# Gate product of the small experts in two weight streams, gathers for two experts at once, and a router in a written order, in a two-layer decoder trunk with a top-2-of-8 expert layer

## Chip, core and metric

The kernel runs on one core of a Trainium2 chip. The metric is the device time of one execution in microseconds (us); the kernel before stands at 1468.9 us, the median of three runs (1468.63 to 1469.94). A change under about 0.2% (2.9 us) can't be told from none.

## The reference, cut to what matters

Two layers over 256 tokens of width 1024 in float32. Each has attention (two head groups) with an output projection `w_out` and a residual, then a feed-forward part: dense SwiGLU in layer 0, top-2-of-8 SwiGLU experts of inner width 3584 in layer 1. The change touches the expert layer and the end of the attention before it:

```python
v = rmsnorm(h, ffn_norm[layer])
h = h + moe_swiglu(v, router_w, exp_w_gate, exp_w_up, exp_w_down)

def moe_swiglu(h, router_w, w_gate, w_up, w_down):
    logits = (hf @ router_w).astype(jnp.float32)
    top_logit, top_e = lax.top_k(logits, TOP_K)
    gate = jax.nn.softmax(top_logit, axis=-1)
    ...
    # each token: the sum over its two experts e of
    #   gate_e * ((silu(x @ w_gate[e]) * (x @ w_up[e])) @ w_down[e])
```

All 8 experts' weights, 336 MiB, are read whatever the routing is. With these inputs four experts (0, 1, 2 and 4) have at most 64 tokens and four (3, 5, 6 and 7) have 65 to 128.

## The kernel before, in words

**Precision.** A float32 operand is split into a rounded part `hi` (type F32R, which TensorE streams in one pass) and a remainder `lo`. A product is then three F32R products: `xh*wh`, `xl*wh`, `xh*wl` (`product3`, lines 406 to 410). The splitting is done on the chip: ScalarE (ACT) writes `whi`, VectorE (DVE) writes `wlo = raw - whi`.

**The weights' stream.** `Flow` (lines 110 to 138) hands the expert layer its weights in 336 pieces of 1 MiB, each 128 x 2048. SyncE's queue (SP) loads them into a ring of `DEEP` = 9 raw buffers (four of tag `raw`, and `x6`, `x5`, `x3`, `x7`, `x4`, which the attention before uses for other things). `flow.hi()` issues the next piece's ACT instruction (line 125), `flow.lo()` the DVE instruction (line 132) and then the load of the piece that takes over the raw buffer. There are 4 `hi` and 3 `lo` buffers.

**Steps.** The expert layer walks through 56 steps, 8 experts by 7 chunks of 512 inner columns, in an order written by hand (`tc.manual_schedule`, from line 1037): each engine executes its instructions in this order. A step (e, c) has six pieces of weights: two halves of the gate, two of the up matrix, and two of the down matrix of the step before. TensorE (PE) computes `eg` (gate) and `eu` (up), ACT takes Silu of `eg`, DVE multiplies (`esg`), PE does the two `down` halves of the step before into `ey`, then turns `esg` (`turn`, tile `eT`), and ACT and DVE split the result into `eth`.

**Few tokens.** A tile has 128 rows. An expert with at most 64 tokens has each token in two slots, s and s + 64. A matmul whose 128 stationary columns are `MIX` = 64:192 of [hi | lo] then has `lo` in the one half and `hi` in the other, so that two matmuls a weight tile (`x_mix*wh`, `x_mix*wl`) take the place of three; the two halves of the result still have to be added. `by_number` (lines 960 to 965) puts both versions into PE's program with a branch on the expert's count. `eu` and `ey` have the two-stream form (lines 979 to 982; `turn` adds the halves with the 0/1 matrix `both`). `eg` always has the three-stream one, because Silu needs the whole sum.

**Gather.** An expert's tokens are gathered by a float32 matmul of a part of `hg` (h times the norm's gain) with the 0/1 matrix `so` (`gather`, lines 894 to 902; 8 column blocks by 2 token tiles, 128 columns each), at chunks 3 and 4 of the expert before; ACT and DVE then split the result into `xe`. `slots`, `rstd_of` and `place` make `so`, the rows' norm factors and the matrix that scatters the results back; finished experts are scattered in pairs (`scatter`, `gain_of`) during the next expert.

**Router.** `to_moe` and its `after` (lines 1211 to 1224) run at the end of the attention, after each column group of the last projection: they turn h (`turn_h`) and write `hg`. `moe` then computes the logits `lg` (lines 833 to 836), the top two (`max`, `max_index`), places by 0/1 matmuls (`rk`, `count`), the norm factors (`row_rstd`), and gathers expert 0. This part's order was found by the scheduler of the framework, and the loads and splits of the first weights run beside it.

Of the kernel before, what the change touches and what calls it, by code (L numbers as in the profile page):

```python
# [21 lines left out]
S = 256  # L22
NT = 2
# [27 lines left out]
DEEP = N_RAW + 5  # L51
# [90 lines left out]
def trunk_kernel(ctx: ExitStack, tc: tile.TileContext, T: dict, out: bass.AP):  # L142
# [81 lines left out]
    later = ("x6", "x5", "x3", "x7", "x4")  # L224
# [604 lines left out]
    def moe(l, mpool, ht, hg):  # L829

        wg = mpool.tile([128, KD, NE], F32, name="wg")
        dve.tensor_tensor(out=wg, in0=wr, in1=column(R_FN + l * KD, KD).unsqueeze(2).to_broadcast([128, KD, NE]), op=ALU.mult)
        lb = [mm_bank("lg")[:, 0:NE] for _ in range(NT)]
        for k in range(KD):
            for t in range(NT):
                pe.matmul(lb[t], ht[:, k, t * 128:(t + 1) * 128], wg[:, k, :], start=(k == 0), stop=(k == KD - 1))

# [3 lines left out]
        for t in range(NT):  # L841
            dve.max(out=mx[:, t, :], in_=lb[t])
            dve.max_index(out=ix[:, t, :], in_max=mx[:, t, :], in_values=lb[t])
        fx = mpool.tile([128, NT, 8], F32, name="fx")
        dve.tensor_copy(fx, ix)
# [5 lines left out]
        one = [mpool.tile([128, NT, NE], F32, name=f"one{i}") for i in range(2)]  # L851
        sel = mpool.tile([128, NT, NE], BF16, name="sel")
        for i in range(2):
            dve.tensor_tensor(out=one[i], in0=ie, in1=per_expert(fx[:, :, i]), op=ALU.is_equal)
        dve.tensor_tensor(out=sel, in0=one[0], in1=one[1], op=ALU.add)

        rb = tr_bank("rk")
        pe.matmul(rb[:, 0:NE], before, sel[:, 0, :], start=True, stop=True)
        pe.matmul(rb[:, NE:2 * NE], ones, sel[:, 0, :], start=True, stop=False)
        pe.matmul(rb[:, NE:2 * NE], before, sel[:, 1, :], start=False, stop=True)  # L860
        pos = mpool.tile([128, NT, NE], F32, name="pos")
        dve.scalar_tensor_tensor(out=pos, in0=rb[:, 0:2 * NE].rearrange("p (t e) -> p t e", t=NT), scalar=1.0, in1=sel,
                                 op0=ALU.add, op1=ALU.mult)


        cb = tr_bank("count")
        for t in range(NT):
            pe.matmul(cb[:, 0:NE], ones, sel[:, t, :], start=(t == 0), stop=(t == NT - 1))
        few = mpool.tile([128, NE], F32, name="few")
        dve.tensor_scalar(out=few, in0=cb[:, 0:NE], scalar1=64.0, scalar2=None, op0=ALU.is_le)  # L870
        number = mpool.tile([128, NE], I32, name="number")
        dve.tensor_copy(number, cb[:, 0:NE])
        most = mpool.tile([128, 1], F32, name="most")
        dve.tensor_reduce(out=most, in_=cb[:, 0:NE], axis=AX.X, op=ALU.max)
        again = tri
        dve.memset(again[:, 0:64], 0.0)
        dve.memset(again[:, 64:128], -64.0)
        both = mpool.tile([128, 128], F32, name="both")
        for i in range(2):
            dve.tensor_tensor(out=both[:, i * 64:(i + 1) * 64], in0=ident[:, 0:64], in1=ident[:, 64:128], op=ALU.add)  # L880
        rs = row_rstd(h, D, "h")

        def slots(e):

            so = mpool.tile([128, NT, 128], F32, name="so", tag="so", bufs=2)
            own = so[:, 0, :]
            dve.scalar_tensor_tensor(out=own, in0=again, scalar=few[:, e:e + 1], in1=slot, op0=ALU.mult, op1=ALU.add)
            for t in reversed(range(NT)):
                dve.tensor_scalar(out=so[:, t, :], in0=own, scalar1=pos[:, t, e:e + 1], scalar2=None,
                                  op0=ALU.is_equal)  # L890
            x = main.tile([128, KD, 2, 128], F32R, name="xe", tag=("ulo", "uhi")[e % 2])
            held[e] = [so, x]

        def gather(e, k):

            so, x = held[e][:2]
            b = tr_bank("ga")
            for j in range(4):
                f = slice((k + j) * 128, (k + j + 1) * 128)
# [11 lines left out]
        def rstd_of(e):  # L911

            so = held[e][0]
            b = tr_bank("rl")
            for t in range(NT):
                pe.matmul(b[:, 0:1], so[:, t, :], rs[:, t:t + 1], start=(t == 0), stop=(t == NT - 1))
            rl = mpool.tile([128, 1], F32, name="rl", tag="rl", bufs=2)
            dve.tensor_copy(rl, b[:, 0:1])
            held[e] += rl, pe.value_load(number[0:1, e:e + 1], min_val=0, max_val=S)
# [3 lines left out]
        slots(0)  # L923
        for k in (0, 4):
            x = gather(0, k)
            upper(*x)
            lower(*x)
        rstd_of(0)
        gt = mpool.tile([128, 2, NT], F32, name="gt")
        dve.tensor_tensor(out=gt[:, 1, :], in0=mx[:, :, 1], in1=mx[:, :, 0], op=ALU.subtract)  # L930
        dve.tensor_tensor(out=gt[:, 1, :], in0=gt[:, 1, :], in1=rs, op=ALU.mult)
        act.activation(gt[:, 1, :], gt[:, 1, :], AF.Exp)
        dve.tensor_scalar(out=gt[:, 0, :], in0=gt[:, 1, :], scalar1=1.0, scalar2=None, op0=ALU.add)
        dve.reciprocal(out=gt[:, 0, :], in_=gt[:, 0, :])
        dve.tensor_tensor(out=gt[:, 1, :], in0=gt[:, 1, :], in1=gt[:, 0, :], op=ALU.mult)
        gte = mpool.tile([128, NT, NE], F32, name="gte")
        for i in range(2):
            dve.tensor_tensor(out=one[i], in0=one[i], in1=per_expert(gt[:, i, :]), op=ALU.mult)
        dve.tensor_tensor(out=gte, in0=one[0], in1=one[1], op=ALU.add)
# [14 lines left out]
        flag = mpool.tile([128, 1], I32, name="flag")  # L954
        dve.tensor_scalar(out=flag, in0=most, scalar1=-128.0, scalar2=0.0, op0=ALU.add, op1=ALU.max)
        over = nc.values_load(flag[0:1, 0:1], min_val=0, max_val=128)

        acc = [mpool.tile([128, D], F32, name=f"acc{t}") for t in range(NT)]

        def by_number(e, many, few):  # L960

            with tc.If(held[e][3] > 64) as cond:
                many()
            with cond.Else():
                few()
# [5 lines left out]
        def terms(e, x, mix, steps):  # L971
# [7 lines left out]
            def few():  # L979
# [9 lines left out]
        def up(e, x, b, half, mix):  # L989
            terms(e, x, mix, [(b, k, wh, wl, k == 0, k == KD - 1) for k, (wh, wl) in enumerate(flow.take(), half * 4)])  # L990

        def down(e, c, ht, y, half):
            terms(e, ht, True, [(y[n], half * 2 + i, wh[:, n * 512:(n + 1) * 512], wl[:, n * 512:(n + 1) * 512],
# [3 lines left out]
        def turn(e, hc):  # L997
# [6 lines left out]
            def few():  # L1004
# [3 lines left out]
            by_number(e, many, few)  # L1008
# [12 lines left out]
        def scatter(c, t, first, pair):  # L1021
            f = slice(c * 512, (c + 1) * 512)
            b = tr_bank("scat")
            for i, (st, yhl) in enumerate(pair):
                for j in range(2):
                    pe.matmul(b, st[:, t * 128:(t + 1) * 128], yhl[:, j, f], start=(i + j == 0), stop=(i + j == 2))
# [9 lines left out]

        with tc.manual_schedule():
            prev = None
            for _ in range(N_HI):
                flow.hi()  # L1040
            for _ in range(N_LO):
                flow.lo()
            for step in seq + [None]:
                e, c = step or (NE, 0)
                if step:
                    _, x, rl, _ = held[e]
                    b = mm_bank("eg")
# [12 lines left out]
                    up(e, x, b, 0, True)  # L1060
                    flow.hi()
                    flow.lo()
                    up(e, x, b, 1, True)
# [3 lines left out]
                if prev:  # L1067
# [6 lines left out]
                    g = None  # L1074
# [3 lines left out]
                    if step:  # L1078
# [4 lines left out]
                    if step:  # L1083
                        lower(ht, b)
                    if g:
                        upper(*g)
                        lower(*g)
                    if pc == last:
                        st, gs = pair[-1]
                        yhl = main.tile([128, 2, D], F32R, name="yhl", tag=f"x{1 + pe_ % 2}")  # L1090
# [200 lines left out]
```

## Time and profile before

| what | before |
|---|---|
| median of 3 runs | 1468.9 us (1468.63 to 1469.94) |
| the profiled execution: its own time / its span | 1466.53 us / 1464.7 us |
| busy PE / DVE / ACT | 97% / 81% / 67% of the span |
| HBM read | 434.45 MB, 297 GB/s over the span |
| chain that ended last | PE 85%, DMA 9%, DVE 3%, ACT 2%, issue 1% |
| granted TensorE clock, mean | 0.993 |

The span runs from the first to the last instruction of the profiled execution. A busy PE is one with matmuls in flight, which is not the same as one at its peak. The expert layer covers the span from about 500 us on. The profile has two records for one float32 matmul, and one for an F32R matmul.

### The profile page before, as it was taken

The page shows a single profiled execution, that of the slowest core. Times are in us where ns is not written, and L with a number is a line of the kernel's source. Part 1 is how long each engine was busy: PE and PEld are TensorE (multiplying, and loading weights), DVE is VectorE, ACT ScalarE, POOL GpSimd, SP SyncE. Part 2 cuts the span into 40 slices and gives each one's busy share as a digit, 9 for nine tenths or more (in the row PEclk, how much of TensorE's full clock was granted, in tenths as well). Part 3 has the DMA queues.
Part 4 walks back from the last instruction along what each step waited for, and adds up shares of the span by engine and source line. Part 5 has one row for each costly group of instructions (what it writes and reads, how often), then busy time and mean ns, then how long its engine had stood idle before and what let it go on. Part 6 is the DMA issues. An engine that isn't in the chain of part 4 may idle for free.

```text
span 1464.7 us, 19495 instructions
## 1 busy us (share of the span) xinstructions
PE 1422.1 (97%) x7166; PEld 1165.2 (80%) x7166; DVE 1190.8 (81%) x1395; ACT 986.8 (67%) x1013; POOL 15.2 (1%) x21
## 2 busy tenths in 40 slices
PE   7999999999999889999999999999999999999997
PEld 6787888888887768877868778888888888888885
DVE  5776755555777679999999998889999888889885
ACT  5556644444665458888788787778787677677773
POOL 2000000000000000000000000000000000000000
PEclk9999999999999889999999999999999999999999
DMA  8922455657725469999999999999999999999990
GB/s 274 315 87 87 144 188 172 218 166 235 251 91 179 150 242 384 395 393 391 394 395 393 393 394 394 393 384 391 393 393 394 384 367 366 326 339 357 365 348 31
DMA packets 201063, 437.72 MB, mean 299 GB/s; under 512 B 9464, under 2 KB 26096, under 8 KB 200944
## 3 DMA queue, kind: packets, MB, share of 16 engines
q1 hardware_dynamic: 198304, 435.16, 81.8%
q8 instruction: 81, 1.33, 0.4%
q10 hardware_dynamic: 2176, 0.52, 0.2%
q0 software_dynamic: 464, 0.40, 0.1%
q14 instruction: 38, 0.31, 0.1%
HBM read 434.45 MB, written 1.08 MB: 297 GB/s over the span
## 4 chain that ended last, share of the span: by engine, by line
PE 85%; DMA 9%; DVE 3%; ACT 2%; issue 1%; SPq 0%; DVEq 0%; ACTq 0%
DMA raw<-in_exp_w_up_dram 7%; PE eg L408 6%; PE eg L410 6%; PE eg L409 6%; PE ey L409 3%; PE ey L410 3%; PE ey L408 3%; PE eu L410 3%; PE eu L409 3%; PE eu L408 3%; PE pj L410 3%; PE pj L408 3%; PE pj L409 3%; PE y L408 2%; PE ey L982 2%; PE eu L981 2%
## 5 line engine op out<-in xcount | busy, mean ns | idle before, releaser
L132 DVE TENSOR_TENSOR wlo<-raw,whi 128x2048 fp32r<-128x2048 f32 x336 | 758.4, 2287 | 56.1 <-PE ey L410 19.4
L125 ACT ACTIVATE whi<-raw 128x2048 fp32r<-128x2048 f32 x336 | 639.1, 1915 | 102.3 <-PE eu L409 26.6
L93 DVE TENSOR_TENSOR wlo<-raw,whi 128x1024 fp32r<-128x1024 f32 (+1 forms) x130 | 154.7, 1193 | 107.2 <-ACT whi L92 102.1
L92 ACT ACTIVATE whi<-raw 128x1024 fp32r<-128x1024 f32 (+1 forms) x130 | 133.5, 1032 | 116.9 <-PE y L409 41.8
L408 PE MATMUL eg<-whi,xe 128*128 128x512 f32 x448 | 181.8, 406 | 0.0
L410 PE MATMUL eg<-wlo,xe 128*128 128x512 f32 x448 | 177.2, 396 | 0.1
L409 PE MATMUL eg<-whi,xe 128*128 128x512 f32 x448 | 177.1, 395 | 0.0
L410 PEld LDWEIGHTS eg<-wlo,xe 128*128 128x128 f32 x448 | 84.2, 188 | 20.7 <-DVE wlo L132 0.5
L409 PEld LDWEIGHTS eg<-whi,xe 128*128 128x128 f32 x448 | 84.4, 188 | 17.8
L408 PEld LDWEIGHTS eg<-whi,xe 128*128 128x128 f32 x448 | 84.4, 188 | 17.6
L982 PE MATMUL ey<-wlo,eth 128*128 128x512 f32 x224 | 89.3, 398 | 2.7 <-DVE wlo L132 2.1
L982 PE MATMUL eu<-wlo,xe 128*128 128x512 f32 x224 | 89.1, 398 | 2.3 <-DVE wlo L132 2.1
L410 PE MATMUL eu<-wlo,xe 128*128 128x512 f32 x224 | 88.7, 396 | 1.2 <-DVE wlo L132 1.2
L981 PE MATMUL eu<-whi,xe 128*128 128x512 f32 x224 | 88.8, 396 | 0.0
L409 PE MATMUL eu<-whi,xe 128*128 128x512 f32 x224 | 88.6, 395 | 0.0
L408 PE MATMUL eu<-whi,xe 128*128 128x512 f32 x224 | 88.6, 395 | 0.0
L408 PE MATMUL ey<-whi,eth 128*128 128x512 f32 x224 | 87.9, 392 | 0.7 <-ACT eth L905 0.7
L981 PE MATMUL ey<-whi,eth 128*128 128x512 f32 x224 | 88.5, 395 | 0.0
L409 PE MATMUL ey<-whi,eth 128*128 128x512 f32 x224 | 87.5, 390 | 0.2 <-DVE eth L908 0.2
L410 PE MATMUL ey<-wlo,eth 128*128 128x512 f32 x224 | 87.5, 391 | 0.0
L905 ACT ACTIVATE eth<-eT 128x512 fp32r<-128x512 f32 x56 | 33.3, 595 | 71.9 <-PE eT L1002 50.2
L408 PE MATMUL pj<-whi,uhi 128*128 128x512 f32 (+1 forms) x192 | 74.7, 391 | 1.6 <-ACT qv L453 1.6
(318 smaller groups left out, 2386.1 us busy)
## 6 DMA issues: line engine op xcount, KB each, us to landing
raw<-in_exp_w_gate_dram SPq DMA_DIRECT2D x112, 1024.0 KB, 11.1
raw<-in_exp_w_up_dram SPq DMA_DIRECT2D x112, 1024.0 KB, 11.3
raw<-in_exp_w_down_dram SPq DMA_DIRECT2D x112, 1024.0 KB, 11.8
raw<-in_w_in_dram SPq DMA_DIRECT2D x20, 1024.0 KB, 6.0
raw<-in_ffn_w_gate_dram SPq DMA_DIRECT2D x10, 1024.0 KB, 5.1
raw<-in_ffn_w_up_dram SPq DMA_DIRECT2D x10, 1024.0 KB, 5.1
raw<-in_ffn_w_down_dram SPq DMA_DIRECT2D x10, 1024.0 KB, 5.0
raw<-in_cmp_w_dram SPq DMA_DIRECT2D x8, 1024.0 KB, 6.0
```

What stands on the lines that cost most here:

```text
L92: self.nc.scalar.activation(hi, src, AF.Copy)
L93: self.nc.vector.tensor_tensor(out=lo, in0=src, in1=hi.bitcast(F32), op=ALU.subtract)
L125: ws.nc.scalar.activation(hi, src, AF.Copy)
L132: self.ws.nc.vector.tensor_tensor(out=lo, in0=src, in1=hi.bitcast(F32), op=ALU.subtract)
L408: pe.matmul(dst, xh, wh, start=first, stop=False)
L409: pe.matmul(dst, xl, wh, start=False, stop=False)
L410: pe.matmul(dst, xh, wl, start=False, stop=last)
L905: act.activation(x[:, :, 0, :], b.rearrange("p (k t) -> p k t", k=4), AF.Copy)
L981: pe.matmul(b, x[:, k, MIX], wh, start=first, stop=False)
L982: pe.matmul(b, x[:, k, MIX], wl, start=False, stop=last)
```

## The change

- The gate has the two-stream form for small experts too. Its two matmuls a weight tile write into one fixed PSUM bank `gp`, cleared once; ACT copies it to `sg`; `whole`, a branch of its own after the first half of `eu`, multiplies `sg` by the 0/1 matrix `both` (float32, 512 columns), which adds the halves; Silu then reads that bank. The copy is issued for every expert, `whole` only runs for small ones.
- The gathers use h times gain split into two F32R parts, `hgh` and `hgl`, instead of a float32 `hg`: 4 matmuls a column block, whose results stand side by side as [hi | lo], so that one ACT copy an expert and block takes the place of the split by ACT and DVE. Experts are gathered in twos (0; 1 and 2; 3 and 4; 5 and 6; 7), 256 columns a matmul, two blocks a step at chunks 3 to 6 of the even experts. A third `xe` buffer takes the tag `x4`, and `DEEP` falls from 9 to 8.
- The router's order is written by hand; the logits' matmuls move to `after`, behind each column group of the last projection; the arithmetic of the experts' weights (`gates`) moves behind the first step; `acc` is `h` itself.
- Expert 6 is scattered by itself during expert 7, and expert 7 alone at the end. In the last step `turn` and its splits stand between the two `down` halves of the step before instead of behind them.

```diff
-DEEP = N_RAW + 5
+DEEP = N_RAW + 4
...
-    later = ("x6", "x5", "x3", "x7", "x4")
+    later = ("x6", "x5", "x3", "x7")
...
+        def slots(es):
+            n = len(es)
+            so = mpool.tile([128, NT, 2, 128], F32R, name="so", tag="so")
...
+                x = main.tile([128, KD, 2, 128], F32R, name="xe", tag=("ulo", "uhi", "x4")[e % 3])
...
+        def gather(pair_, k):
...
+            b = tr_bank("ga").rearrange("p (i e t) -> p i e t", i=2, e=2)
+            f = slice(k * 128, (k + 1) * 128)
+            for i in range(2):
                 for t in range(NT):
-                    pe.matmul(b[:, j * 128:(j + 1) * 128], hg[:, t, f], so[:, t, :], start=(t == 0), stop=(t == NT - 1))
-            return x[:, k:k + 4], b
+                    pe.matmul(b[:, i, 0:n, :], hg[i][:, t, f], so[:, t], start=(t == 0), stop=(t == NT - 1))
+            for i, x in enumerate(xs):
+                act.activation(x[:, k], b[:, :, i, :], AF.Copy)
...
-        def terms(e, x, mix, steps):
+        def terms(e, x, steps, part=None):
...
+            def fewer():
                 for b, k, wh, wl, first, last in steps:
+                    b = b if part is None else part
                     pe.matmul(b, x[:, k, MIX], wh, start=first, stop=False)
                     pe.matmul(b, x[:, k, MIX], wl, start=False, stop=last)
-            if mix:
-                by_number(e, many, few)
-            else:
-                many()
...
+            by_number(e, many, fewer)
...
+        def whole(e, b, part):
+            with tc.If(held[e][4] > 0):
+                pe.matmul(b, both, part, start=True, stop=True)
...
+        def router():
+            rstd = rstd_steps()
+            squares()
...
+            flow.hi()
+            flow.hi()
...
+            first_ = slots([0])
+            for k in range(4):
+                gather(first_, k)
+            next(rest)
+            flow.hi()
+            flow.lo()
+            next(rest)
+            for k in range(4, KD):
+                gather(first_, k)
+            for _ in rstd:
+                pass
+            flow.lo()
...
+            rstd_of(0)
...
+            flow.lo()
+            act.activation(gt[:, 1, :], gt[:, 1, :], AF.Exp)
+            flow.hi()
...
+            router()
+            gp = cmp_bank("gp")
+            dve.memset(gp, 0.0)
...
-                    up(e, x, b, 0, False)
+                    up(e, x, g, 0, gp)
                     flow.hi()
                     flow.lo()
-                    up(e, x, b, 1, False)
+                    up(e, x, g, 1, gp)
                     sg = mpool.tile([128, 512], F32, name="esg", tag="esg")
-                    act.activation(sg, b, AF.Silu, scale=rl)
+                    act.activation(sg, gp, AF.Copy)
...
-                    up(e, x, b, 0, True)
+                    up(e, x, b, 0)
+                    whole(e, g, sg)
+                    act.activation(sg, g, AF.Silu, scale=rl)
...
-                    if step and e + 1 < NE and c in (3, 4):
-                        g = gather(e + 1, (c - 3) * 4)
+                    final = step == seq[-1]
+                    if final:
+                        nxt, b = turn(e, sg)
+                        upper(nxt, b)
+                        lower(nxt, b)
+                    if step and e % 2 == 0 and c >= 3:
+                        for k in range((c - 3) * 2, (c - 2) * 2):
+                            gather(coming, k)
                     down(pe_, pc, ht, y, 1)
...
-                        if pe_ % 2:
+                        if pe_ % 2 or pe_ == NE - 2:
                             left.extend((n, t, pe_ == 1, pair) for n in range(2) for t in range(NT))
...
+                    if (e, c) == (0, 0):
+                        gates()
...
+                    if c == 2 and e % 2 == 0:
+                        coming = slots([i for i in (e + 1, e + 2) if i < NE])
...
             def after(c0, cw):
                 turn_h(c0, cw, ht)
-                f = slice(c0, c0 + cw)
-                for t in range(NT):
-                    dve.tensor_tensor(out=hg[:, t, f], in0=h[t][:, f], in1=row[:, f], op=ALU.mult)
+                for k in range(c0 // 128, (c0 + cw) // 128):
+                    for t in range(NT):
+                        pe.matmul(lb[t], ht[:, k, t * 128:(t + 1) * 128], wg[:, k, :], start=(k == 0), stop=(k == KD - 1))
+                if c0 + cw <= 512:
+                    list(scaled(slice(c0, c0 + cw)))
```

`scaled` is the split of h times gain: two DVE products and two ACT copies, then two DVE subtractions; for the second half of the columns `router` issues them (`next(rest)`).

## Rows read from the trace of the kernel before

**Rows 1.** Stretches: busy us (PE, PEld, DVE, ACT, POOL), PE clock, DMA share, GB/s

```profile
510.00:520.00 10.00, 2.82 (x18) 2.73 (x17) 8.76 (x39) 0.45 (x2) 0.00 (x0) 0.50 0.60 211
...
530.00:540.00 10.00, 7.96 (x38) 6.29 (x38) 8.37 (x6) 7.39 (x5) 0.00 (x0) 1.00 1.02 376
540.00:550.00 10.00, 10.00 (x52) 8.36 (x50) 9.26 (x6) 8.51 (x7) 0.00 (x0) 1.00 0.90 323
...
720.00:850.00 130.00, 126.33 (x583) 100.21 (x583) 124.58 (x79) 103.33 (x70) 0.00 (x0) 1.00 1.04 393
...
960.00:1080.00 120.00, 120.00 (x573) 99.45 (x572) 117.43 (x76) 97.48 (x67) 0.00 (x0) 1.00 1.04 389
...
1250.00:1300.00 50.00, 50.00 (x240) 41.28 (x239) 41.36 (x29) 33.35 (x25) 0.00 (x0) 1.00 0.93 326
```

**Rows 2.** Tile eu by line: L981 is the two-stream form, L408 the other

```profile
L981 PE MATMUL eu<-whi,xe x224: 390/398/496, 528.7 to 1069.8; 128*128 128x512 f32 x112
...
L408 PE MATMUL eu<-whi,xe x224: 392/394/398, 848.4 to 1439.4; 128*128 128x512 f32 x112
```

**Rows 3.** The chain that ended last, 740 to 1100 us: start, us, what

```profile
848.70 13.94 DMA raw<-in_exp_w_up_dram
...
967.21 0.44 PE eT L1002 x4
...
988.92 0.93 PE scat L1026 x4
...
1074.10 0.89 PE eT L1006 x8
```

**Rows 4.** The same chain, 1100 to 1436 us

```profile
1158.00 1.78 PE ga L901 x16
...
1411.54 0.44 PE eT L1002 x4
1428.63 0.44 PE eT L1002 x4
```

**Rows 5.** Groups of ACT, 540 to 1440 us: count, busy us, mean ns, idle before

```profile
L905 ACT ACTIVATE eth<-eT 128x512 fp32r<-128x512 f32 x54 | 32.1, 595 | 67.1 <-PE eT L1002 46.0 <-PE eT L1006 21.1
...
L949 ACT ACTIVATE st<-pl 128x256 fp32r<-128x256 f32 x8 | 3.0, 372 | 0.0
```

**Rows 6.** Timeline of SP's queue around the router

```profile
528.44 3.18 SPq L74 DMA_DIRECT2D raw<-in_exp_w_up_dram  x2
```

**Rows 7.** Timeline around the router and the first step: start, us, instructions

```profile
497.76 0.28 PE L410 MATMUL y<-wlo,pob 128*128 128x256 f32 x1
497.88 0.28 PE L408 MATMUL y<-whi,pob 128*128 128x256 f32 x1
...
503.29 6.74 PE L836 MATMUL lg<-wg,ht 128*128 128x8 f32 x32 [1.01 <-DVE wg L832]
...
515.34 0.17 DVE L855 TENSOR_TENSOR sel<-one,one 128x16 bf16<-128x16 f32 x1
...
517.49 5.30 PE L901 MATMUL ga<-so,hg_rows 128*128 128x128 f32 x32 [1.64 <-DVE y_h L324]
...
522.99 0.48 PE L408 MATMUL eg<-whi,xe 128*128 128x512 f32 x1
...
528.44 0.40 PE L410 MATMUL eg<-wlo,xe 128*128 128x512 f32 x1
528.67 0.39 PE L981 MATMUL eu<-whi,xe 128*128 128x512 f32 x1
```

**Rows 8.** Timeline of DVE, early in expert 0

```profile
546.80 6.68 DVE L132 TENSOR_TENSOR wlo<-raw,whi 128x2048 fp32r<-128x2048 f32 x3
```

**Rows 9.** The chain that ended last, its end: start, us, what

```profile
1446.83 0.70 DVE eth L908
...
1454.20 3.43 PE scat L1026 x13
...
1457.66 0.69 DVE acc L1030
```

More of the change, by code (lines that the diff above doesn't have):

```diff
@@ L826, in ffn, with moe @@
         return hi, lo
[L829 to L834, printed above, removed]
-            for t in range(NT):
-                pe.matmul(lb[t], ht[:, k, t * 128:(t + 1) * 128], wg[:, k, :], start=(k == 0), stop=(k == KD - 1))
+    def moe(l, mpool, lb, hg, rest):
         mx = mpool.tile([128, NT, 8], F32, name="mx")
         ix = mpool.tile([128, NT, 8], U32, name="ix")
-        for t in range(NT):
-            dve.max(out=mx[:, t, :], in_=lb[t])
-            dve.max_index(out=ix[:, t, :], in_max=mx[:, t, :], in_values=lb[t])
         fx = mpool.tile([128, NT, 8], F32, name="fx")
-        dve.tensor_copy(fx, ix)
+        one = [mpool.tile([128, NT, NE], F32, name=f"one{i}") for i in range(2)]
+        sel = mpool.tile([128, NT, NE], BF16, name="sel")
+        pos = mpool.tile([128, NT, NE], F32, name="pos")
+        few = mpool.tile([128, NE], F32, name="few")
+        number = mpool.tile([128, NE], I32, name="number")
+        small = mpool.tile([128, NE], I32, name="small")
+        most = mpool.tile([128, 1], F32, name="most")
+        flag = mpool.tile([128, 1], I32, name="flag")
+        both = mpool.tile([128, 128], F32, name="both")
+        gt = mpool.tile([128, 2, NT], F32, name="gt")
+        gte = mpool.tile([128, NT, NE], F32, name="gte")
+        acc = h
+        again = tri
         ie = iota.unsqueeze(1).to_broadcast([128, NT, NE])
@@ L849, in per_expert @@
             return v.unsqueeze(2).to_broadcast([128, NT, NE])
[L851 to L899, printed above, removed]
+        ss = main.tile([128, NT], F32, name="ss", tag="ss_h", bufs=2)
+        rs = main.tile([128, NT], F32, name="y_h", tag="rs_y_h", bufs=2)
+        def squares():
+            for t in range(NT):
+                junk = main.tile([128, D], BF16, name="junk", tag="junk")
+                act.activation(junk, h[t], AF.Square, accum_out=ss[:, t:t + 1])
@@ L918, in rstd_of @@
             dve.tensor_copy(rl, b[:, 0:1])
-            held[e] += rl, pe.value_load(number[0:1, e:e + 1], min_val=0, max_val=S)
+            held[e] += (rl, pe.value_load(number[0:1, e:e + 1], min_val=0, max_val=S),
+                        pe.value_load(small[0:1, e:e + 1], min_val=0, max_val=1))
         held = {}
[L923 to L939, printed above, removed]
         def place(e):
@@ L952, in place, with by_number @@
             return st, gs
[L954 to L960, printed above, removed]
+        def by_number(e, many, fewer):
             with tc.If(held[e][3] > 64) as cond:
@@ L1037, in moe, with gates @@
+        def gates():
+            dve.tensor_scalar(out=gt[:, 0, :], in0=gt[:, 1, :], scalar1=1.0, scalar2=None, op0=ALU.add)
+            dve.reciprocal(out=gt[:, 0, :], in_=gt[:, 0, :])
+            dve.tensor_tensor(out=gt[:, 1, :], in0=gt[:, 1, :], in1=gt[:, 0, :], op=ALU.mult)
+            for i in range(2):
+                dve.tensor_tensor(out=one[i], in0=one[i], in1=per_expert(gt[:, i, :]), op=ALU.mult)
+            dve.tensor_tensor(out=gte, in0=one[0], in1=one[1], op=ALU.add)
         with tc.manual_schedule():
+            pool.memset(again[:, 0:64], 0.0)
+            pool.memset(again[:, 64:128], -64.0)
@@ L1082, in moe @@
                     flow.lo()
-                    if step:
+                    if step and not final:
                         lower(ht, b)
-                    if g:
-                        upper(*g)
-                        lower(*g)
                     if pc == last:
                         st, gs = pair[-1]
-                        yhl = main.tile([128, 2, D], F32R, name="yhl", tag=f"x{1 + pe_ % 2}")
+                        yhl = (mpool if pe_ % 2 else main).tile([128, 2, D], F32R, name="yhl", tag="x1")
                         weigh(gs, y, yhl, False)
```

131 lines of the change are left out of this document (98 added, 33 removed).

## The prediction

> **What bounds the kernel now.** The change lies almost wholly in the expert layer, so I read that stage by stage, first by stretches of time, then along the chain of work that ended last.
>
> The stretches [rows 1] show three regimes. From 720 to 850 us (experts 1 and 2, small) the DMA engines are full at 393 GB/s, while PE idles 4 and DVE 5 us of 130. A piece of 1 MiB takes 1.0486 MB / 393 GB/s = 2.67 us there, a step of six 16.0 us. From 960 to 1080 us (about expert 4) PE is busy 120.0 of 120 us and DVE 117.4: two engines full at once, with the DMA near full. From 1250 us on only PE is full, and the DMA falls to 326 GB/s. The tile of the up product tells which experts are which [rows 2]: the two-stream line has 224 hi products, four experts' worth, until 1070 us; the three-stream one has 224 from 848 us to the end. So the gate change applies to experts 0, 1, 2 and 4 only.
>
> The chain has its last DMA link at 848.70 + 13.94 = 862.6 us [rows 3], at the start of expert 3. What happens before shifts the end only by shifting the weights' stream; behind it the chain is PE's, down to the tail, so that work taken from PE there counts in full, unless DVE or DMA fills the place. The steps there: a plain one of a large expert lasts 1428.63 - 1411.54 = 17.09 us [rows 4], of which `turn` has 0.44, so each of its 72 products takes 16.65 / 72 = 0.231 us. A half gather costs 1.78 us (16 records, 8 float32 matmuls of 128 columns, 0.111 a record); the chain holds two for each expert fetched. Expert 4 reaches from the turn at 967.21 to that at 1074.10, 106.9 us [rows 3].
>
> **The change part by part.** The sum is made against the profiled execution (1466.53 us, span 1464.7); the median of the runs is 2.4 us higher, and I carry the difference over to it.
>
> *Experts 0 to 2.* The gate loses 8 of 24 products a step, 8 x 0.231 = 1.85 us, and gains `whole`, 512 float32 columns, the work of the eight records of a small expert's `turn`: 0.89 us [rows 3]. Net -0.96 us of PE a step. ACT gains a copy of 128x512, 0.60 us as for `eth` [rows 5]. The limit here is the DMA, at 16.0 us a step, so this is worth nothing by itself; the same goes for the gathers in these experts and for DVE's two fewer splits an expert.
>
> *When the stream starts.* A DMA-bound stretch ends earlier only if it starts earlier. Before, the thirteenth piece goes out at 528.44 [rows 6], when the split behind the first half gate frees a buffer. For the new router I add up the chain. The logits: 12 of their 16 products move ahead of the projection's end; 32 records took 6.74 us at half clock [rows 7], so 12 products cost about 6.74 x 12/16 / 2 = 2.5 us at full clock, in a PE stream that has no room for them (256-column products follow each other 0.12 us apart [rows 7]). The 4 that stay behind cost 1.3 us (between 0.85 at full and 1.7 at half clock). From their end to `sel` the old order has two splits of 2.23 us each [rows 8] which the new one has not: 515.34 - 510.03 + 0.17 = 5.5 us become 1.1. From `sel` to the first gather product it is 517.49 - 515.51 = 2.0 us, as before. So gathering starts at about 517.49 + 2.5 - (6.74 - 1.3) - 4.4 = 510.2. But DVE then has in order: two products and two subtractions of 512 columns (0.70 each, as for `eth` [rows 9]), three splits (2.23 each), some 15 small instructions of 0.17 [rows 7] and the clearing of `gp` (taken as 0.5): 12.5 us, and `eg` waits for the last. First gate product: 522.7, against 522.99 [rows 7]. [...] The half gate then has 8 products (1.9 us at full, 3.7 at half clock; 2.6 taken), the split 2.3: the load goes out at 527.6. With 8 buffers, though, that is the twelfth piece, not the thirteenth, so the stream is 527.6 + 2.67 - 528.44 = 1.8 us behind. Some of it comes back: from 530 to 550 us the DMA ran at 376 and 323 GB/s [rows 1], 2.2 us short of full, as PE needed 12 products for a half gate; with 8, DVE's pace rules, which is under 2.67 us a piece but for the short first step. I take **+1.5 us**, bounds -1.5 (a router 1 us shorter and all of the startup loss regained) and +4 (half clock throughout the first gate, nothing regained).
>
> *Expert 3.* Its two half gathers move into expert 2, under the DMA: -2 x 1.78 = **-3.6 us**.
>
> *Expert 4.* PE's work falls by 56 x 0.231 = 12.9, rises by 7 x 0.89 = 6.2, loses 3.6 of gathers and gains those for 5 and 6, 32 matmuls of 256 columns at 0.12 = 3.8: -6.5 us in all. But DVE was at 117.43 of 120, or 97.9% [rows 1], and its work hardly changes (two splits fewer, one set of `slots` more). So at most 2.1% of 106.9 = 2.3 us can come back. ACT, at 97.48 of 120 = 86.8 us of the 106.9, gains seven copies (4.2) and 16 gather copies of 128x256 (0.37 each [rows 5]) for two of 0.60: 95.8 of 105, or 91%. **-1.5 us**, bounds -2.3 and +2 for ACT's in-order waits. The DMA allows it: experts 3 and 4 would take 7 x 17.09 + 105.4 = 225.0 us, and 84 pieces need 224.1; more than a microsecond beyond it would be the DMA's again.
>
> *Expert 5.* The gathers for expert 6 are done in expert 4: **-3.6 us**.
>
> *Expert 6.* The 16 float32 matmuls for expert 7 (3.6 us) become 32 F32R ones of 128 columns, a form the trace lacks. Below 0.111 us they hardly go: the nearest rows, 128 columns a record, are spaced so [rows 4]. Above, 0.223 if F32R at this width costs as much as float32. I take 0.111, the spacing at equal columns: 3.6, so **0**, bounds 0 and +3.6. [...]
>
> *Expert 7.* Scattering expert 6 by itself puts 8 products here, four of which take 0.93 us [rows 3]: **+1.8 us**, fully on PE.
>
> *The tail.* Before, PE waits for ACT and DVE to split the last `eth` (0.60 + 0.70 [rows 5, 9]); with `turn` moved ahead of a `down` half, 12 products of 0.23 = 2.8 us cover that: -1.3. The last scatter has 8 products instead of 16: behind the first split of the result, 3.43 + 0.69 us [rows 9] become one more split and four additions on DVE, 5 x 0.69 = 3.45: -0.7. Together **-2.0 us**, bounds -2.4 and 0.
>
> *Costed at nothing:* the copy and the later Silu in large experts (ACT is busy 33.35 of 50 us [rows 1], and Silu is done a half `eu`, 2.8 us, before DVE needs it); the loss of a buffer, once the stream runs; `acc` in h; and the branches, in large experts three more a step. The cover for these is that PE's sequencer runs ahead: across the branch ahead of `eu`, the next product follows after 528.67 - 528.44 = 0.23 us, like any other [rows 7].
>
> Sum: 1.5 - 3.6 - 1.5 - 3.6 + 0 + 1.8 - 2.0 = -7.4 us: 1459.1 for the profiled execution, **1461.5 us** for the median.
>
> **The rivals.**
>
> *Added branches cost PE time (slower).* Place: the 28 steps of large experts, 3 new branches each, 84. Price: if PE's queue runs dry at each, a product costs its own 0.39 us instead of 0.23 [rows 7], 0.16 x 84 = 13.4 us: 1474.9. It decides from (7.4 + 2.9) / 84 = 0.12 us a branch. Against it: the five branches of each step now cost nothing visible. For it: a longer program, and the very first gate hangs on a freshly loaded register. [...] So far the trace speaks against it. Chance 0.08.
>
> *ACT becomes the bound in expert 4.* At 91% with waits on PE in its order (the copy, Silu behind `whole`, the gather copies ahead of the next turn), it may fall back to the DMA's pace, 7 x 16.0 = 112 us instead of 105.4: +6.6, 1468.1, no change. Against it: in DMA-bound steps it is several pieces ahead. 0.10.
>
> *The stream starts late.* PE comes to the gate cold, 16 products at half clock, and nothing is regained: +6 instead of +1.5, 1466.0 to 1469, no change. 0.10. Both losses together: about 1473, slower, 0.04.
>
> *The stream starts early.* If the logits fit into PE's gaps and DVE's list is shorter than I added up, the stream gains 3 to 4 us: 1456 to 1457. 0.11.
>
> **How the numbers follow.** The forecast (1457 to 1466) has 0.57. Faster by over 0.2% (below 1466.0): 0.57 + 0.11 = 0.68. Within 0.2%: 0.10 + 0.10 = 0.20. Slower: 0.08 + 0.04 = 0.12. That 0.2% is about what a measurement can tell from no change. The range reaches from 1454 (all terms at their lower bounds are -1.5 - 3.6 - 2.3 - 3.6 + 1.8 - 2.4 = -11.6, and a little of the early case) to 1471, which takes in both no-change cases.
>
> **What would show it.** In the profile of the changed kernel: the first `eg` product near 523 us and the DMA full from about 530 to 860; no gather in expert 3 or 5, and steps of 17.1 us there; PE no longer full in expert 4, DVE above 97%; gather products of expert 7 spaced 0.11 us; no wait for `eth` in the tail. I am wrong if steps of large experts are longer than 17.1 us without a gather or scatter in them (branches), if DMA runs below 390 GB/s from 720 to 850 us (the small experts slipped), or if the first gate product is at 518 or 528 us.

## The result, and the profile after

| | before | after |
|---|---|---|
| median of 4 runs each, same chip | 1469.2 us | 1490.9 us (1487.7 to 1491.5) |
| ratio, 95% interval | 1 | 1.0143 (1.0125 to 1.0160) |
| profiled execution: time / span | 1466.53 / 1464.7 us | 1491.45 / 1489.6 us |
| busy PE / DVE / ACT | 97% / 81% / 67% | 95% / 80% / 69% |

The change makes the kernel 1.4% slower; I had forecast 1461.5 us. It is 22 us by the medians and 24.9 by the two profiled spans, with which the working below is done.

Stretches of the changed kernel, with the columns of [rows 1]:

```profile
530.00:550.00 20.00, 18.87 (x82) 14.30 (x81) 18.86 (x17) 18.79 (x15) 0.00 (x0) 1.00 0.83 288
...
720.00:850.00 130.00, 116.51 (x496) 88.97 (x497) 120.56 (x79) 106.82 (x87) 0.00 (x0) 0.96 1.04 394
836.00:843.00 7.00, 7.00 (x24) 5.86 (x24) 3.31 (x4) 4.20 (x4) 0.00 (x0) 0.51 1.04 390
...
960.00:1080.00 120.00, 116.52 (x526) 90.55 (x525) 115.25 (x77) 101.79 (x85) 0.00 (x0) 1.00 1.02 380
1110.00:1400.00 290.00, 284.93 (x1267) 226.67 (x1266) 241.76 (x144) 208.79 (x157) 0.00 (x0) 1.00 0.98 349
```

Two things are new. From 1110 to 1400 us PE now idles 5 of 290 us. The kernel before has no idle PE there:

```profile
1110.00:1400.00 290.00, 290.00 (x1331) 237.73 (x1330) 249.83 (x152) 207.37 (x140) 0.00 (x0) 1.00 1.00 361
```

And near the end of expert 2, from 836 to 843 us, the granted clock falls to 0.51, with the DMA still full at 390 GB/s. (A shorter drop, to 0.55 for 3.4 us from 730 us on, is in the row from 720 to 850 too.)

The middle of `eu` in a large expert shows where PE stops. Timeline of the changed kernel, PE and ACT (start, duration, instruction, in brackets the idle time before it and what ended it):

```profile
1398.47 0.60 PE L980 MATMUL eT<-cc,esg 128*128 128x128 f32 x4
...
1404.98 0.40 PE L408 MATMUL eu<-whi,xe 128*128 128x512 f32 x1
...
1407.56 0.39 PE L410 MATMUL eu<-wlo,xe 128*128 128x512 f32 x1
...
1408.14 0.69 ACT L1105 ACTIVATE esg<-eg,rl 128x512 f32<-128x512 f32 x1 [1.01 <-PEq L967]
...
1408.26 0.49 PE L408 MATMUL eu<-whi,xe 128*128 128x512 f32 x1 [0.31 <-PEq L967]
1408.59 0.40 PE L409 MATMUL eu<-whi,xe 128*128 128x512 f32 x1
...
1411.16 0.40 PE L408 MATMUL ey<-whi,eth 128*128 128x512 f32 x1
...
1416.77 0.60 PE L980 MATMUL eT<-cc,esg 128*128 128x128 f32 x4
```

From the last product of the first half to the first of the second it is 0.70 us, and 0.33 to the one behind it, instead of 0.233 each: 0.57 us lost. The product is released by PE's own sequencer at line 967, the branch of `whole`. The instructions of that line (duration min/median/max in ns, first and last start), and who waited for them (us, times):

```profile
L967 PEldq COMPARE_BRANCH  x84: 70/176/293, 528.4 to 1457.8; - x84
L967 PEldq EVENT_SEMAPHORE  x28: 51/51/51, 863.4 to 1462.0; - x28
...
  ACT esg L1105: 21.1, 28
  DVE wlo L132: 9.3, 18
  PE eu L408: 8.8, 28
```

Of the 84 branch records 56 are the compare, one a step, and 28 the small experts' jump over the other path. The semaphore instruction stands in 28 steps, those of the large experts, which skip the arm. The built program (PE's part, shortened) says what it is:

```
L967 compare and branch
L968 matmul eg<-esg,both 128x512      [waits for ACT; adds 1 to PE's count]
L967 jump to the end
L967 semaphore instruction            [waits for PE's count; adds 1 to it]
L967 jump to the end
```

The last two lines are the skipped path. PE's count is what other engines' instructions wait for; ACT's Silu waits for line 967 in all 28 of these steps (21.1 us above). The skipped path has no product to add to it, so the program that the framework builds lets the sequencer add the 1, and first wait until PE's last product is done. In the step shown the semaphore instruction starts at 1408.0 us; the last product of the first half ends at 1407.56 + 0.39 = 1407.95. The other branches (`by_number`) have products in both arms and no such wait: across the one ahead of `ey` in this step the next product follows after 0.23 us (1410.93 to 1411.16).

The step as a whole: from the turn at 1398.47 to that at 1416.77 us it is 18.30 us with two scatter products, 17.85 without, against 17.09 [rows 4]. The skip is 0.57 of the 0.76. Of the other 0.19, `ey` has 0.15: its 24 products take 5.61 us (1411.16 to 1416.77), 0.234 each; before they took 5.46, 0.227 each:

```profile
1423.01 0.39 PE L408 MATMUL ey<-whi,eth 128*128 128x512 f32 x1
...
1428.47 0.60 PE L1002 MATMUL eT<-cc,esg 128*128 128x128 f32 x4
```

### The profile page after: what moved, and what is told of

Read it like the earlier page. It is cut to its first block, busy times and chain, and to the rows that moved or that the text cites. A ratio compares the mean times of both kernels' runs of the same rounds, so it can differ in the third digit from the quotient of the medians.

```text
span 1489.6 us, 19492 instructions
## 1 busy us (share of the span) xinstructions
PE 1412.3 (95%) x6902; PEld 1123.8 (75%) x6902; DVE 1188.1 (80%) x1385; ACT 1026.5 (69%) x1121; POOL 15.3 (1%) x23
## 5 line engine op out<-in xcount | busy, mean ns | idle before, releaser
L957 PE MATMUL eu<-whi,xe 128*128 128x512 f32 x224 | 100.8, 450 | 0.0
L408 PE MATMUL eu<-whi,xe 128*128 128x512 f32 x224 | 91.5, 408 | 8.8 <-PEq L967 8.8
L957 PE MATMUL gp<-whi,xe 128*128 128x512 f32 x224 | 93.5, 417 | 4.7 <-DVE gp L1085 3.3
L958 PE MATMUL gp<-wlo,xe 128*128 128x512 f32 x224 | 91.7, 409 | 0.5
L408 PE MATMUL eg<-whi,xe 128*128 128x512 f32 x224 | 91.0, 406 | 0.0
L408 PE MATMUL ey<-whi,eth 128*128 128x512 f32 x224 | 89.0, 398 | 0.7 <-ACT eth L901 0.7
L409 PE MATMUL eg<-whi,xe 128*128 128x512 f32 x224 | 88.8, 396 | 0.0
L410 PE MATMUL eg<-wlo,xe 128*128 128x512 f32 x224 | 88.7, 396 | 0.0
L409 PE MATMUL eu<-whi,xe 128*128 128x512 f32 x224 | 88.6, 396 | 0.0
L408 PE MATMUL pj<-whi,uhi 128*128 128x512 f32 (+1 forms) x192 | 74.7, 391 | 1.6 <-ACT qv L453 1.6
L410 PE MATMUL pj<-wlo,uhi 128*128 128x512 f32 (+1 forms) x192 | 74.3, 388 | 0.8 <-DVE wlo L93 0.8
```

What stands on the lines that cost most here:

```text
L408: pe.matmul(dst, xh, wh, start=first, stop=False)
L409: pe.matmul(dst, xl, wh, start=False, stop=False)
L410: pe.matmul(dst, xh, wl, start=False, stop=last)
```

## The experiments

The first four ask what the 0.57 us is, and what is left without it. "The first kernel" in an expectation is that of experiment 1.

**1. The 0/1 product in an arm that exists.** The branch of `whole` and the one inside `eu` ask the same question, so the product can stand in the two-stream arm of the first half of `eu`:

```diff
             def fewer():
                 for b, k, wh, wl, first, last in steps:
                     ...
+                if then is not None:
+                    pe.matmul(then[0], both, then[1], start=True, stop=True)
 ...
-                    up(e, x, b, 0)
-                    whole(e, g, sg)
+                    up(e, x, b, 0, None, (g, sg))
```

> Theory A (the skipped arm of the 0/1 product ends in a jump that waits until PE has finished its last product; 28 skips, about 0.57 us each): the gap of 0.71 us in the middle of eu is gone, a plain step of a large expert is 17.28 us instead of 17.85, the time 1491 - 16 = 1475 us. Rival C (the large steps are longer because Silu comes a half eu later and holds ACT): Silu is as late here, so steps stay at 17.85 us and the time at about 1491 us.

Measured: 1475.4 us, ratio 1.0051 (1.0034 to 1.0068). The steps of large experts are 17.28 us; chain that ended last, and the middle of `eu`:

```profile
1419.06 0.44 PE eT L982 x4
1436.34 0.44 PE eT L982 x4
```

```profile
1427.29 0.40 PE L409 MATMUL eu<-whi,xe 128*128 128x512 f32 x1
1427.53 0.40 PE L410 MATMUL eu<-wlo,xe 128*128 128x512 f32 x1
1427.77 0.39 PE L408 MATMUL eu<-whi,xe 128*128 128x512 f32 x1
```

Theory A by the numbers: 15.5 us of the 22 were this wait. Silu is as late as in the changed kernel, so rival C is out.

**2. The branch stays, its other arm gets a product.**

```diff
-            with tc.If(held[e][4] > 0):
+            with tc.If(held[e][4] > 0) as cond:
                 pe.matmul(b, both, part, start=True, stop=True)
+            with cond.Else():
+                pe.matmul(spare[:, 0:8], both, ident[:, 0:8], start=True, stop=True)
```

> Here the branch stays, and its other arm has a product of 8 columns (into a bank that nobody needs in a large expert). Theory A: no jump that waits for PE is left, so only the 8-column product is paid, some 0.1 us a step: large steps 17.3 to 17.4 us, time 1475 to 1479 us. Rival B (every added branch costs PE its queue, whatever is in its arms): large steps stay at 17.8 us or more, time 1491 us or more.

Measured: 1479.7 us, ratio 1.0090 (1.0071 to 1.0109), steps of 17.48 us. The branch's compare is there, the semaphore instruction is gone; behind it two turns of the chain that ended last:

```profile
L967 PEldq COMPARE_BRANCH  x84: 70/176/328, 528.3 to 1445.5; - x84
```

```profile
1423.30 0.44 PE eT L982 x4
...
1440.78 0.44 PE eT L982 x4
```

Step and time lie just above what I expected: the small product costs 0.2 us a step rather than 0.1. But most of the 0.57 is gone with the branch still in place. Rival B, the full price at every branch, is out.

**3. A branch that is always skipped, for a product that nobody needs.** On top of experiment 1, where `whole` stood:

```diff
+        def never(e, b):
+            with tc.If(held[e][3] > 250):
+                pe.matmul(b[:, 0:8], both, ident[:, 0:8], start=True, stop=True)
```

> The product of the small experts is in the arm of eu, as in the first kernel, and where the branch stood is one that is skipped in all 56 steps and whose product no engine ever needs. Theory A: 28 waits of 0.57 us come back in the large experts, those of the small ones hide under the weights' stream: 1491 us, steps 17.85 us, although ACT waits for nothing there. If the loss lay in ACT's wait for the skipped product (rival C), this runs like the first kernel, about 1475 us.

Measured: 1490.9 us, the time of the changed kernel, with its 17.85 us steps; on the same chip that is 15.6 us above experiment 1. Waits of the profile (us, times, longest):

```profile
ACT esg L1107 <- PEq L969: 26.3, 38, 2.1
PE eu L957 <- PEq L969: 12.3, 26, 0.6
...
PE eu L408 <- PEq L969: 8.8, 28, 0.3
```

The wait comes back, now in small experts too (26 times, line 957). There the weights' stream hides most of it: expert 2 ends at 848.3 us, in experiment 1 at 848.6, where the granted clock was 0.57 from 834 to 842 us; expert 4 takes 0.7 us longer than there. So the price is one of skipping, whether or not the product is ever needed.

**4. The gate in three streams again,** everything else as changed: `gp`, the copy and `whole` are out, Silu reads `eg`.

> The gate in three streams for all experts again; router, gathers, scatter and 8 buffers as changed. Theory A with its three smaller losses (28 x 0.57 = 16 us of skips; 3.4 us of half clock in expert 2 because PE has too little to do there with a two-stream gate; 4.8 us because the products of down are spaced 0.2333 instead of 0.2265 us): skips and clock drop go, 1491 - 16 - 3.4 = 1471 to 1472 us, less 4.8 if the spacing hangs on the gate too; expert 4 gains nothing from it (DVE). Rival D (router and gathers cost as much as the gate): the time stays above 1478 us.

Measured: 1477.7 us, ratio 1.0070 (1.0054 to 1.0087). The steps are 17.28 us, as in experiment 1. What I expected of the rest failed: `ey` stays slow, so the gate is not its cause; the clock still falls in expert 2, to 0.57 from 802 to 806 us; and the stream falls behind by 2 us more at its start, where PE has three products a tile again. Expert 4 takes 110.9 us instead of 108.4. The time is close to the 1478 of rival D: most of what is left above the kernel before is not the gate's.

**5 to 7. Why `ey` is slower.** The rows of all kernels so far have F32R products of 512 columns at two spacings, in long stretches at 0.2267 or about 0.2333 us, and which one it is goes with the operands, not with the time. The tiles' addresses in the built programs differ: before, `eth` and the split weights begin at 32 modulo 128 bytes and `xe` at 96; after, the weights at 0, `eth` at 64, `xe` at 96 (modulo 256 the figures are the same). The dense products earlier in the kernel, at 0.2267, have both operands at 96. The edits, on top of experiment 1, are unused bytes, `pad1` 96 of them ahead of the split weights and `pad2` 64 ahead of `eth`:

```diff
+        mpool.tile([128, 24], F32, name="pad1", tag="pad1")
         acc = h
 ...
             router()
+            mpool.tile([128, 16], F32, name="pad2", tag="pad2")
```

`pad2` alone:

> As the first kernel (whole in the arm, 1475.4 us), with 64 unused bytes ahead of eth, so that eth begins at the same place modulo 128 bytes as the split weights (before: both at 32; after: 64 against 0). Theory E (a product is spaced 0.2267 us where weights and moving operand begin at the same place modulo 128 bytes, 0.2333 where not): ey goes back to 0.2267, eg and eu stay at 0.2333, a plain large step is 17.28 - 24 x 0.0067 = 17.12 us, the time 1475.4 - 4.5 = 1471 us. Rival F (the spacing of ey hangs on what ACT, DVE and the DMA do beside it): ey stays at 0.2333, steps 17.28, 1475 us.

Measured: 1474.3 us, ratio 1.0041 (1.0027 to 1.0055), steps of 17.25 us: theory E with 128 bytes fails here. Both:

> As the first kernel, with 96 bytes ahead of the weights' buffers and 64 ahead of eth: xe, eth and the split weights now all begin at 96 modulo 128 bytes. Theory E: all 72 products of a large step at 0.2267, a plain step 17.28 - 72 x 0.0067 = 16.80 us, the time 1475.4 - 28 x 0.48 = 1462 us or a little less (where DVE or the DMA do not become the bound: a step of the DMA is 16.0 us). Rival F: no change from 1475 us.

Measured: 1466.4 us, ratio 0.9987 (0.9977 to 0.9997), steps of 16.95 us. In its timeline, the first product of `eu`, of `ey`, and the turn:

```profile
1415.87 0.39 PE L408 MATMUL eu<-whi,xe 128*128 128x512 f32 x1
...
1421.32 0.40 PE L408 MATMUL ey<-whi,eth 128*128 128x512 f32 x1
...
1426.90 0.60 PE L983 MATMUL eT<-cc,esg 128*128 128x128 f32 x4
```

24 products of `eu` in 5.45 us (0.227), 24 of `ey` in 5.58 (0.2325): the weights with `xe` did what was expected, those with `eth` did not. In both kernels `eth` lay 128 bytes off modulo 256; `xe` did not in the second. With 192 bytes ahead of `eth` instead of 64 (`pad1` left out):

> The run with 64 bytes ahead of eth changed ey too little (spacing 0.2315 us), while the one that also moved the weights brought eg and eu to 0.2267: so the period is not 128 bytes. All pairs seen so far fit a period of 256 bytes (0.2267 where weights and moving operand begin at the same place modulo 256, 0.2333 at a distance of 64 or 96, 0.2315 at 128). This is the first kernel (whole in the arm) with 192 unused bytes ahead of eth, which then begins at 0 modulo 256, as the split weights do. Theory E with 256 bytes: ey at 0.2267, a plain large step 17.12 us, 1471 us. If the place does not rule ey (rival F), 17.25 us and 1474.5 us.

Measured: 1471.3 us, ratio 1.0016 (1.0005 to 1.0028), steps of 17.13 us:

```profile
1423.70 0.39 PE L408 MATMUL eu<-whi,xe 128*128 128x512 f32 x1
...
1429.32 0.39 PE L408 MATMUL ey<-whi,eth 128*128 128x512 f32 x1
...
1434.79 0.49 PE L982 MATMUL eT<-cc,esg 128*128 128x128 f32 x3
```

Now `ey` takes 5.47 us (0.228) and `eu` 5.62 (0.234): the reverse. So the spacing goes with the distance of the two operands modulo 256 bytes. The distances come from the built programs, the times of 24 products in plain steps from the traces:

| kernel | `xe` and weights, bytes: `eu`, us | `eth` and weights, bytes: `ey`, us |
|---|---|---|
| before | 64: 5.60 | 0: 5.46 |
| experiment 1 | 96: 5.62 | 64: 5.60 |
| `pad2` alone | 96: 5.62 | 128: 5.58 |
| both | 0: 5.45 to 5.49 | 128: 5.58 |
| 192 bytes | 96: 5.62 | 0: 5.47 |
| experiment 8 | 0: 5.44 | 0: 5.45 |

Other distances were not tried. In the changed kernel no one touched `ey`; other tiles grew and shrank ahead of it, and its place moved.

**8. The same bytes in the kernel before.** 64 unused bytes at the start of the expert layer's tiles, nothing else:

```diff
+        mpool.tile([128, 16], F32, name="pad1", tag="pad1")
         wg = mpool.tile([128, KD, NE], F32, name="wg")
```

> The kernel before the change with nothing but 64 unused bytes at the start of the expert layer's tiles, so that xe, eth and the split weights all begin at 96 modulo 256 (before: xe at 96, the others at 32). Theory E: eg and eu at 0.2267 as ey is already, a plain large step 17.09 - 48 x 0.0067 = 16.77 us, 28 of them: 1468.8 - 9 = 1460 us. Rival F: 1468.8 us.

Measured: 1459.0 us, ratio 0.9933 (0.9919 to 0.9948), steps of 16.81 us (chain):

```profile
1404.88 0.44 PE eT L1003 x4
...
1421.69 0.44 PE eT L1003 x4
```

**9. The clearing of `gp`.** In the changed kernel the first gate product waits for it, and it stands behind a split on DVE:

```profile
522.76 2.29 DVE L132 TENSOR_TENSOR wlo<-raw,whi 128x2048 fp32r<-128x2048 f32 x1
...
525.15 0.48 DVE L1085 MEMSET gp<- 128x512 f32 x1
525.69 0.80 PE L957 MATMUL gp<-whi,xe 128*128 128x512 f32 x1 [3.32 <-DVE gp L1085]
```

The edit moves the two lines that take and clear the bank to behind `sel`, on top of experiment 1.

> As the first kernel, with the clearing of gp (0.48 us on DVE, which the first gate product waits for) moved to where DVE waits for PE in the router. If the stream of weights starts late because of DVE's list, the first gate product comes 0.5 us earlier and so does everything to the end: 1475 us. If the order of the router is bound elsewhere (gathers at half clock), nothing moves: 1475.4 us. The bound on what a start of the stream is worth stays the 3.5 us by which the kernel without gp began its gate earlier.

Measured: 1472.6 us, ratio 1.0027 (1.0017 to 1.0038) against 1.0051 (1.0034 to 1.0068). From the projection's end to the first gate product it is 18.1 us instead of 20.0: 1.9 us, not 0.5, because the split no longer stands ahead of the clearing.

**10. The last `eth`.** In the changed kernel its split starts only when the second `down` half is done:

```profile
1470.97 0.40 PE L410 MATMUL ey<-wlo,eth 128*128 128x512 f32 x1
1471.41 0.60 ACT L901 ACTIVATE eth<-eT 128x512 fp32r<-128x512 f32 x1 [4.37 <-PE ey L410]
```

That half reads the one `eth` tile. Here the last one has a tile of its own, on top of experiment 1:

```diff
+            if spare:
+                return main.tile([128, KD, 2, 128], F32R, name="eth", tag="ulo")[:, 0:4], b
             return mpool.tile([128, 4, 2, 128], F32R, name="eth", tag="eth"), b
```

> As the first kernel, but the last eth gets a tile of its own (the place of the xe of expert 6, no longer read). Theory: turn was moved ahead of the second half of down, but its split could not start, since the one eth tile was still being read by that half; with a tile of its own the waits of 1.08 and 0.73 us behind turn go, and the tail is 1.3 to 1.8 us shorter: 1473.8 us. Rival (the last scatter sets the end of the tail whatever comes before it): 1475.4 us.

Measured: 1472.7 us, ratio 1.0030 (1.0021 to 1.0040). ACT now starts right behind `turn`, and the tail (from the last `esg`) is 21.8 us instead of 23.5:

```profile
1449.11 0.60 PE L982 MATMUL eT<-cc,esg 128*128 128x128 f32 x4
...
1449.74 0.60 ACT L901 ACTIVATE eth<-eT 128x512 fp32r<-128x512 f32 x1 [1.56 <-PE eT L982]
```

This execution shows something else by chance: the clock did not fall. Two stretches of experiment 1, then of this one:

```profile
834.00:842.00 8.00, 7.48 (x26) 6.13 (x27) 4.39 (x4) 4.82 (x5) 0.00 (x0) 0.57 1.04 393
```

```profile
834.00:842.00 8.00, 6.38 (x33) 5.38 (x34) 6.00 (x6) 6.51 (x10) 0.00 (x0) 1.00 1.04 393
```

The last step of expert 2 took 19.51 us there and 16.96 here: the drop cost 2.5 us. (In experiment 2, with a mean clock of 0.992 over the span against 0.988 in experiment 1, that step took 16.68 us.)

**11. The ninth buffer,** taken out of the kernel before (`DEEP = N_RAW + 4`, `x4` out of the list):

> The kernel before with 8 raw buffers instead of 9, and nothing else. Theory G (in a stream that the DMA bounds from the first piece that it has to wait for a buffer, one buffer less puts every later piece back by one, 2.67 us, and nothing of it comes back): piece 30 lands at 584.6 instead of 581.9 us, the end 2.7 us later, 1471.8 us. Theory H (my forecast: a part is regained while the stream runs below its full rate at 530 to 550 us): under 1.5 us, 1470.3 us or less.

Measured: 1471.2 us, ratio 1.0023 (1.0011 to 1.0035). The load that waits for the first half gate goes out when it did before [rows 6], but it is the twelfth:

```profile
528.41 0.37 SPq L74 DMA_DIRECT2D raw<-in_exp_w_gate_dram  x1
```

Piece 30 (counted from 0; bytes summed over the trace's DMA records) lands at 584.6 instead of 581.9 us. Nothing is regained: theory G.

**12, 13. All together,** with the two-stream gate and with the three-stream one (1, 9, 10, `pad1` and 192 bytes ahead of `eth`):

> Everything together on the changed kernel: the 0/1 product in the arm of eu, xe, eth and weights at 96 modulo 256, gp cleared early, a tile of its own for the last eth. Large step 16.80 us; from the run with all at 96 modulo 128 (1466.4 us), less 28 x 24 x 0.005 = 3.3 us for ey, 1.7 for the tail, 1 to 2 for the early clearing: 1460 us.

> The same with the gate in three streams again (no gp, no 0/1 product). What the gate change is worth by itself, without its branch: by the two runs before, 1475.4 with and 1477.7 without, the two-stream gate gives about 2 us, mostly in expert 4 (108.4 against 110.9 us) and less a drop of PE's clock in expert 2. Expected 1462 us, 2 us above the kernel beside it. If the two-stream gate is worth nothing once PE is not the bound of a small expert, the two are within 1 us.

Measured: 1459.2 us, ratio 0.9931 (0.9919 to 0.9943), and 1462.0 us, ratio 0.9946 (0.9933 to 0.9959). The first has steps of 16.82 us:

```profile
1406.53 0.44 PE eT L983 x4
...
1423.35 0.44 PE eT L983 x4
```

It is faster than both kernels. But 64 unused bytes give the kernel before the same time (experiment 8): with its faults mended, the change comes to no gain over the old kernel with its operands in the same places. The gate itself is worth 2.9 us here, at intervals that overlap; that is hardly more than a measurement can tell.

## Why the prediction was wrong

The step that failed is "Costed at nothing", and in it the branches. Its cover, that PE's sequencer runs ahead, was read off a branch with products in both arms, and it holds for two of the three new branches a step, those of the gate: experiments 1 and 4, with them and without, have the same step of 17.28 us. `whole` has one arm. The rival for slower had the right place (the large experts) and nearly the right sum, 13.4 us against 28 x 0.57 = 16.0, for another reason: not 0.16 us at each of 84 branches, but a full wait at 28. That the sums are near is luck. In the trace of the changed kernel the compare at line 967 lasts 70 ns where PE goes on into the arm and 207 to 218 where it skips it, and the jump behind the arm 169 to 180 (once 293). Neither is the price: in the step shown that is the 0.70 us from product to product across the skip and the 0.33 behind it, instead of 0.233 each.

Term by term, in the profiled spans (+24.9 against -7.4, 32.3 us off):

- *Skips:* 16.0 us, costed at 0.
- *Spacing of products:* 28 x 0.19 = 5.3 us, mostly in `ey`. No step had it, since the change of place was not in the list of what a changed tile does.
- *The stream's start:* piece 138 lands 433.3 us after the first load's issue, before 429.4: +3.9, where I took +1.5 with a bound of +4. The logits cost 3.2 us inside the projection (46.3 instead of 43.0 us; I had 2.5 and no room); the router from there is 2.2 us shorter (20.1 instead of 22.2), held back by the clearing of `gp`; the buffer costs its full 2.7, of which I had hoped for a part back. The first gate product, at 525.7 us, was neither at 523 nor at 528; 1.6 us of it are a later start of this execution: the first of the experts' loads goes out at 442.9 instead of 441.3 us, and the executions shown here scatter from 440.2 to 445.3. No run shows the 2.6 us taken for the first half gate, a choice between full and half clock: in the changed kernel it takes 3.5 us (525.69 to 529.15), at a granted clock of 0.50 from 525.7 to 528.4 us.
- *End of expert 2:* it falls 3.5 us further behind the stream (from piece 120 to its last `esg` 21.7 us, before 18.2). The gathers for expert 3, which I put "under the DMA", stand there. By experiments 1 and 10 about 2 of it are the clock drop, and the rest stays without it (19.9); that this rest is the gathers' is not shown. PE's idle share was wanted in the sum as cover; that the granted clock may fall just before PE becomes the bound, to 0.51 from 836 to 843 us, was not in it. Before it was 1.00 there.
- *Experts 3 and 5:* less their seven skips and slower products (5.3 us each) they are 2.8 and 2.3 us shorter, against 3.6 and 3.6. *Expert 4:* 1.5, as forecast; DVE is busy 106.6 of 108 us there. *Expert 6:* 1.1 shorter, forecast 0; its gather products are spaced 0.11 us, as taken (8 in 0.84 us, from 1339.67 to 1340.51). *Expert 7:* 2.6 longer, forecast 1.8. Together 5 us of gain instead of 6.9.
- *Tail:* -0.3 instead of -2.0. The move of `turn` was read as if the split behind it needed only PE and ACT; its target was in use. Experiment 10 gives the -1.7.
- *Start of the execution:* +1.6, not the change's.

The misses are 16.0 + 5.3 + 2.4 + 3.5 + 1.9 + 1.7 + 1.6 = 32.4, which is the 32.3 within rounding. The sign of "DMA below 390 GB/s" was not seen (394), and the one that I had named for the branches, steps above 17.1 us, was. In the aligned kernels (experiments 8 and 12) experts 4 and 5 save 2.6 us together, forecast 5.1. Most of the rest stands between the last `esg` of expert 4 and the first of expert 5, 16.12 us instead of 14.47: there PE does the last two gather blocks (0.95 us) and `turn` waits for their copies, which ACT does behind three splits of weights. Experiment 12:

```profile
1076.16 1.16 PE L987 MATMUL eT<-both,esg 128*128 128x128 f32 x8 [0.53 <-ACT xe L899]
```

This is a small piece of the rival that had ACT as the bound in expert 4. What stays open: where the last 1 us or so of these two experts goes, and why the clock falls in expert 2 of one execution and not of another whose instructions there are the same.

## What to carry to other kernels

In a program built as here, a branch cost PE nothing visible where both paths have a product of PE that is needed anyway (0.23 us to the next one), and 0.57 us where one path has none and ends in a wait until PE is done; other engines were not tried. Put optional work into an arm that exists. When tiles are added or removed, compare the addresses of the operands of the hottest instruction before and after; here 64 bytes in the old kernel were worth as much as the change with all its mends. Work moved ahead of its consumer also needs its output buffer free there (1.7 us of the tail, experiment 10).

## What the runs showed of the hardware

- F32R products of 512 columns are spaced 0.227 to 0.229 us where the 128 stationary columns and the moving operand begin at the same place modulo 256 bytes, 0.2325 to 0.234 at a distance of 64, 96 or 128 (kernels before and after, experiments 5 to 8). Why is not shown.
- A skipped arm with nothing of PE in it, for which the built program has the sequencer wait, costs PE 0.57 us at full clock (experiments 1 to 3). Across a branch with products in both arms the next product follows after 0.24 us (experiment 1, the middle of `eu`), as without one.
- A granted clock of 0.57 from 834 to 842 us, just as PE becomes the bound, went with a last step of expert 2 that was 2.5 us longer than in another execution, where it was 1.00 (experiments 1 and 10).
